# A hand-ordered passage from the O projection into the up projection of a float32 decoder layer

## The chip, the cores and the metric

One NeuronCore of one Trainium2 chip runs the program. The metric is the device time of one execution in microseconds (us); a time of a kernel is the median of its runs. Engines are named as the profile names them: PE (TensorE, matmuls), DVE (VectorE), ACT (ScalarE), POOL (GpSimd), SP (SyncE, which issues all DMAs here).

## What is computed

One layer of a decoder in float32, 1024 tokens by 1024 channels. Cut to what matters:

```python
def reference(x, ...):
    h = x
    u = rms_norm(h, attn_norm)
    h = h + swa_mixer(u, w_qkv, sinks, w_o)      # windowed attention; ends in "o @ w_o", the O projection
    u = rms_norm(h, mlp_norm)                    # statistics over the channels of each token
    a = jax.nn.relu(u @ w_up)                    # w_up 1024 x 4096, the up projection
    h = h + (a * a) @ w_down                     # the down projection
    return rms_norm(h, final_norm)
```

## The kernel before

Activations lie transposed: 8 tiles `h[m]` of 128 channels by 1024 tokens, and the tokens are taken in two halves of 512 columns. Every float32 matmul is made of three: an operand is split into a rounded part (`_h`, a copy on ACT) and a rest (`_l`, a subtraction on DVE), and `mm3b` multiplies high by high, high by low and low by high into one PSUM bank.

**The O projection's second part** runs 16 blocks (8 channel tiles by 2 halves) of 12 matmuls. After each block DVE adds it into `h[m]`, ACT squares the result, and POOL (tiles 1 to 4) or DVE (tile 5) adds up the squares. `stat_sum(hf)` sums them over channels with small matmuls (`n2s`) and makes the reciprocal root (`n_st`, ACT and DVE) and a diagonal tile `dg`; `stat_bcast(hf)` spreads it over the partitions with a matmul (`n2b`). Half 0 is normed while half 1 is still projected (`norm_first`, giving `x1_i` and its split `xb`).

**The up projection** uses a seven-product scheme (Winograd's form of Strassen's) on 2 by 2 blocks: the columns of `w_up` are taken as 16 pairs `p`, and for each the products 1 to 7 of weight terms and activation terms are formed (`TERM`). A product (n, p) is four channel groups i of three matmuls. Products 1 and 2 need only half 0 (`xb`). The others need the terms `t1` and `t2` (`ta`, split into `xt`), `t3` and `t4` (split into `xu`) and `b22` (split into `xc`), which mix both halves: per group i, `norm_second` norms the two tiles of half 1 into a new tile (two scalar_tensor_tensor), subtracts twice for `ta`, splits it, has POOL make the two differences for t3 and t4 in place of `x1_i`, and splits `xc`. Weight sums (`sa`, `sb`) come from POOL (`up_sums`), their splits `ws`, `wb`, `wt` from `up_splits`.

Results are taken out of PSUM after most products: (1,p) and (6,p) are copied by ACT, (2,p) is added by DVE into `oa` and squared-relu'd (`relu2`, one DVE instruction), and so on; each result is stored to DRAM (`hid`) by SP. PSUM has three banks X, two Y, one Z and two mm: (1), (6), (7), (4) of one p share a bank X, (5) and (3) a bank Y, (2) a bank Z.

**What sets the order.** The matmuls are always in program order (`pe.ordered`). DVE, ACT and POOL are ordered by hand only through the attention (`Ordered`); from there on the build's scheduler places their instructions, by program order as priority and by its own estimate of when each is ready. Each engine then runs its list strictly in turn. Tiles come from small pools (tags A 16 tiles, Q 8, O 6, W 6, K 4, R 3 for raw weights, t4 6 for temporaries, sq 4), and an instruction that needs a slot waits until its last reader is done. The products run as (1,0), (2,0), (1,1), (2,1), (1,2), (2,2), (1,3), (2,3), (6,0), (5,0), (6,1), (5,1), (7,0), (6,2), (4,0), (3,0), (7,1), (5,2), (6,3), (4,1), (3,1) and so on. Line 41, which nearly all rows carry, is the `Ordered` wrapper, so rows are told apart by their tiles.

Of the kernel before, what the change touches and what calls it, by code (L numbers as in the profile page):

```python
# [62 lines left out]
def trunk(tc, xT, gains, wqkv, wo, wup, wdn, bias_d, sinks_d, ident_d, mask_d, outT):  # L63
# [602 lines left out]
    def xalloc(dt, name):
        return xslots.pop(0)(dt, name)

    def norm_second(i, rb):
# [5 lines left out]
        for m in (2 * i, 2 * i + 1):
            d = nc.sync.dma_start(hd[m], h[m])
            tc.add_manual_dep(d.ins, stt.ins.name, mybir.DependencyInfo(
                mybir.DependencyClass.Sync, mybir.DependencyReason.DATA), reason="order")
# [6 lines left out]
        XP["b22", i] = split1(xt[:, 1], xalloc, f"xc{i}")  # L685

    def norm_third(i):
        XP["t3", i], XP["t4", i] = split2(x1[i], xalloc, f"xu{i}")

    def ring():  # L690
        tags, n = [wtile] * 6 + [otile] * 6, [0]
# [36 lines left out]

    PS, OUT = {}, {}
# [6 lines left out]
    def up_product(n, p):  # L736
# [21 lines left out]
        if n == 1:
            s.copy(c11, ps)
        elif n == 2:  # L760
            v.tensor_tensor(c11, ps, c11, op=ALU.add)
            relu2(c11, c11)
            store(2, c11)
        elif n == 6:
            s.copy(OUT["b", p][:, 0], ps)
# [40 lines left out]
    for hf in range(2):
        for m in range(KT):
            ps = bank(obanks[(hf * KT + m) % 5], f"o1_{m}_{hf}")
            for kk in range(4):
                mm3(ps, wsl(ws[m // 2], (m % 2) * 4 + kk), o_t[4 + kk], HALVES[hf], kk == 0, kk == 3)  # L810
            v.tensor_tensor(h[m][:, HALVES[hf]], ps, h[m][:, HALVES[hf]], op=ALU.add)
            square(m, hf)
            if hf == 1 and m == 1:
                stat_sum(0)
            if hf == 1 and m == 3:
                rb = stat_bcast(0)
            if hf == 1 and m > 3:
                norm_first(m - 4, rb)
# [220 lines left out]
```

## Time and profile before

| | |
|---|---|
| median of 3 runs | 956.98 us (955.43 to 957.41) |
| the profiled execution's own time | 957.42 us, its span 955.7 us |
| PE busy | 920.7 us of the span (96%) |
| DVE, ACT, POOL busy | 689.4, 441.3, 313.1 us |

The profile has one page (busy times, the span in 40 slices of 23.9 us, the costliest groups) and views asked of the trace: a timeline of one engine (start, duration, what was done, and in brackets how long the engine sat idle before and who released it), groups of instructions, and busy times of chosen stretches. The attention ends near 249 us, the O projection's second part at 296 us, the up projection near 633 us, and the down projection follows. A matmul's duration overlaps the next one's, so its price is the distance from start to start.

### The profile page before, as it was taken

The page shows a single profiled execution, that of the slowest core. Times are in us where ns is not written, and L with a number is a line of the kernel's source. Part 1 is how long each engine was busy: PE and PEld are TensorE (multiplying, and loading weights), DVE is VectorE, ACT ScalarE, POOL GpSimd, SP SyncE. Part 2 cuts the span into 40 slices and gives each one's busy share as a digit, 9 for nine tenths or more (in the row PEclk, how much of TensorE's full clock was granted, in tenths as well). Part 3 has the DMA queues.
Part 4 walks back from the last instruction along what each step waited for, and adds up shares of the span by engine and source line. Part 5 has one row for each costly group of instructions (what it writes and reads, how often), then busy time and mean ns, then how long its engine had stood idle before and what let it go on. Part 6 is the DMA issues. An engine that isn't in the chain of part 4 may idle for free.

```text
span 955.7 us, 12587 instructions
## 1 busy us (share of the span) xinstructions
PE 920.7 (96%) x4500; PEld 772.5 (81%) x4500; DVE 689.4 (72%) x947; ACT 441.3 (46%) x837; POOL 313.1 (33%) x266
## 2 busy tenths in 40 slices
PE   7999999999999859999999999999999999999996
PEld 5778888888887647888888888878888888888995
DVE  6779988989746886776657665555868697467963
ACT  8478878777533343433333333333343333455510
POOL 4116656566361265544544454110000000030100
PEclk9999999999998969999999999999999999999998
DMA  8200100510410424555345533799898989447722
GB/s 301 69 23 28 56 27 8 204 45 25 153 45 23 167 100 174 176 168 170 126 144 169 173 127 140 260 311 390 292 328 312 341 327 342 131 132 246 282 89 88
DMA packets 56174, 160.36 MB, mean 168 GB/s; under 512 B 6320, under 2 KB 10160, under 8 KB 56112
## 3 DMA queue, kind: packets, MB, share of 16 engines
q1 hardware_dynamic: 56112, 159.57, 47.4%
q8 instruction: 35, 0.57, 0.2%
q14 instruction: 27, 0.22, 0.1%
HBM read 121.79 MB, written 37.75 MB: 167 GB/s over the span
## 4 chain that ended last, share of the span: by engine, by line
PE 60%; DVE 1%; POOL 1%; issue 0%; ACT 0%; DVEq 0%; ACTq 0%; POOLq 0%
PE d L41 32%; PE uX L41 15%; PE uY L41 8%; PE uZ L41 3%; POOL sa L41 0%; POOL sb L41 0%; DVE out L41 0%; PE n L41 0%; PE n3b L41 0%; DVE wb L41 0%; DVE hr L41 0%; DVE ws_l L41 0%; ACT oc L41 0%; ACT ws_h L41 0%; ACT wt_h L41 0%
## 5 line engine op out<-in xcount | busy, mean ns | idle before, releaser
L41 PE MATMUL d<-dx_h,dw_h 128*128 128x512 f32 (+1 forms) x512 | 186.8, 365 | 1.0 <-DVE hr L41 1.0
L41 PE MATMUL d<-dx_l,dw_h 128*128 128x512 f32 (+1 forms) x512 | 185.9, 363 | 0.0
L41 PE MATMUL d<-dx_h,dw_l 128*128 128x512 f32 (+1 forms) x512 | 185.9, 363 | 0.0
L41 PEld LDWEIGHTS d<-dx_h,dw_h 128*128 128x128 f32 x512 | 96.7, 189 | 16.6 <-DVE hr L41 1.4
L41 PEld LDWEIGHTS d<-dx_l,dw_h 128*128 128x128 f32 x512 | 96.7, 189 | 15.2 <-issue 0.2
L41 PEld LDWEIGHTS d<-dx_h,dw_l 128*128 128x128 f32 x512 | 96.7, 189 | 15.0
L41 ACT CAST dw_h<-wf 128x1024 fp32r<-128x1024 f32 x40 | 42.1, 1053 | 112.4 <-PE d L41 64.9
L41 POOL TENSOR_TENSOR ssq3a<-ssq3a,sq_a 128x512 f32<-128x512 f32 x7 | 10.8, 1544 | 212.9 <-ACT sq_a L41 212.5
L41 DVE TENSOR_TENSOR dx_l<-hr,dx_h 128x1024 fp32r<-128x1024 f32 x56 | 70.3, 1256 | 6.1 <-ACT dx_h L41 6.1
L41 DVE TENSOR_TENSOR dw_l<-wf,dw_h 128x1024 fp32r<-128x1024 f32 x40 | 49.2, 1231 | 27.3 <-ACT dw_h L41 27.3
L41 POOL TENSOR_TENSOR t<-t,sm 128x512 f32<-128x512 f32 x32 | 33.3, 1041 | 102.9 <-DVE sm L41 102.9
L41 DVE TENSOR_TENSOR wf<-wd,we 128x1024 f32<-128x1024 f32 x40 | 48.3, 1221 | 25.0 <-DMA we<-wdn 17.5
L41 ACT CAST dx_h<-hr 128x1024 fp32r<-128x1024 f32 x56 | 58.6, 1047 | 10.9 <-DMA hr<-hid 6.3
L41 ACT ACTIVATE t<-t,sm 128x129 f32<-128x129 f32 x128 | 50.5, 397 | 11.0 <-DVE sm L41 10.5
L41 PE MATMUL f<-xh,w_h 128*128 128x512 f32 x128 | 53.7, 420 | 0.0
L41 PE MATMUL f<-xl,w_h 128*128 128x512 f32 x128 | 50.9, 397 | 0.0
L41 PE MATMUL f<-xh,w_l 128*128 128x512 f32 x128 | 50.5, 395 | 0.0
L41 ACT COPY oa<-uX 128x512 f32<-128x512 f32 x32 | 18.8, 587 | 61.1 <-PE uX L41 61.1
L41 POOL TENSOR_TENSOR ob<-ob,oa 128x512 f32<-128x512 f32 x16 | 20.6, 1289 | 80.4 <-DVE ob L41 80.4
L41 POOL TENSOR_TENSOR oc<-oc,oa 128x512 f32<-128x512 f32 x16 | 22.6, 1411 | 69.4 <-DVE oc L41 69.4
L41 PE MATMUL uX<-xu_h,wb 128*128 128x512 f32 x128 | 42.2, 391 | 0.7 <-ACT oa L41 0.7
L41 DVE TENSOR_TENSOR oc<-oc,oa 128x512 f32<-128x512 f32 x16 | 13.0, 813 | 38.1 <-ACT oc L41 38.0
(341 smaller groups left out, 2454.5 us busy)
## 6 DMA issues: line engine op xcount, KB each, us to landing
wd<-wdn SPq DMA_DIRECT2D x56, 512.0 KB, 6.0
hr<-hid SPq DMA_DIRECT2D x56, 512.0 KB, 4.9
we<-wdn SPq DMA_DIRECT2D x40, 512.0 KB, 6.8
hid<-oa SPq DMA_DIRECT2D x32, 256.0 KB, 3.0
hid<-oc SPq DMA_DIRECT2D x32, 256.0 KB, 2.3
hid<-ob SPq DMA_DIRECT2D x32, 256.0 KB, 2.3
w_r<-wqkv SPq DMA_DIRECT2D x8, 512.0 KB, 3.9
h<-xT SPq DMA_DIRECT2D x8, 512.0 KB, 6.4
```

Of the source, the lines that this page charges most:

```text
L41: ins = method(*args, **kw)
```

## The change

- From the second half of the O projection's blocks to the product (6,2), DVE, ACT and POOL run in program order; the program order there is rewritten line by line, with the split of a tile into its `_h` copy and its `_l` subtraction placed apart.
- `stat_sum(0)` comes one block after the first half's last (it was two), `stat_bcast(0)` one block later (it was three), and the four `norm_first` steps two or more blocks before the end. `stat_sum(1)` is put inside product (1,0), after its third group, and `stat_bcast(1)` inside (2,0), after its third.
- `second_half` norms half 1 in place of `h`, so `h` is stored to `hd` before, in 16 stores of half a tile rather than 8.
- The differences for t3 and t4 go from POOL to DVE and come after all `ta`. The relu and square of (2,0) to (2,3) go from one DVE instruction to two on ACT, after product (5,1). The `xc` splits come after the ordered part.
- `wb` of p 0 and 1 is split ahead of the O projection; the weight sums of p 2 are made in place of the raw weights and one `sq` tile, ahead of the products; those of p 3 come with (7,1). Tags of some tiles change.
- The products' order from (6,2) on is (6,2), (7,0), (7,1), (4,0), (3,0), (5,2), (4,1), (6,3), (3,1), (7,2), (5,3), (4,2), (3,2), (7,3), (1,4), (4,3), (2,4), (3,3); from p 4 on it is unchanged.

No matmul is added or taken away. The core of the diff is below. In it `his` makes the `_h` copy on ACT and returns the function that makes the `_l` subtraction on DVE; `t34(i)` and `t34_lo(i)` do the same for `xu` of group i; `c11_add` is DVE's addition of (2,p) into `oa`; `snapshot` is ACT's copy of (1,p) or (6,p); `up_mms` is a product's matmuls alone, with functions called after given groups.

```diff
+    def second_half(i, rb):
+        for m in (2 * i, 2 * i + 1):
+            hm = h[m][:, HALVES[1]]
+            v.scalar_tensor_tensor(hm, hm, gn[:, 1, m:m + 1], rb, op0=ALU.mult, op1=ALU.mult)
+    def t_sums(i):
+        ta = (temp if i < 2 else lambda n: two(atile(F32, n)))(f"ta{i}")
+        v.tensor_tensor(ta[:, 1], h[2 * i][:, HALVES[1]], x1[i][:, 0], op=ALU.subtract)
+        v.tensor_tensor(ta[:, 0], h[2 * i + 1][:, HALVES[1]], ta[:, 1], op=ALU.subtract)
+        return ta
-        g.tensor_tensor(x1[i][:, 0], ta[:, 0], x1[i][:, 0], op=ALU.subtract)
-        g.tensor_tensor(x1[i][:, 1], x1[i][:, 1], ta[:, 0], op=ALU.subtract)
+    def t3_sum(i):
+        v.tensor_tensor(x1[i][:, 0], TA[i][:, 0], x1[i][:, 0], op=ALU.subtract)
+    def t4_sum(i):
+        v.tensor_tensor(x1[i][:, 1], x1[i][:, 1], TA[i][:, 0], op=ALU.subtract)
+    def c11_relu(p):
+        c11 = OUT["a", p][:, 0]
+        s.activation(c11, c11, AF.Relu)
+        s.activation(c11, c11, AF.Square)
+        store(2, p, c11)
...
+    for e in (v, s, g):
+        e.ordered = True
+    for m in range(KT):
+        ps = oblock(m, 1)
+        if m == 1:
+            rb = stat_bcast(0)
+        if 2 <= m < 5:
+            LO[m - 1] = first_half(m - 1, rb)
+        if 2 <= m < 6:
+            XP["b11", m - 2], XP["b21", m - 2] = LO[m - 2]()
+        if m == 6:
+            WU["s2", 0], WU["s1", 0] = LO["ws0"]()
+        oadd(m, 1, ps)
+        if m == 0:
+            stat_sum(0)
...
+        if m == 1:
+            LO[0] = first_half(0, rb)
+        if m == 5:
+            LO["ws0"] = his(SUM[0][1], wtile, "ws0")
+        if m == 6:
+            LO["wt0"] = his(SUM[0][2], wtile, "wt0")
...
+    s2_2 = up_sums_inplace(2, *u2)
+    WU["s3", 0], WU["s4", 0] = LO["wt0"]()
+    up_mms(1, 0, {2: lambda: stat_sum(1)})
+    LO["wa3"] = his(wu3, ktile, "wa3")
+    snapshot(1, 0)
+    WU["a11", 3], WU["a12", 3] = LO["wa3"]()
+    bc = []
+    up_mms(2, 0, {2: lambda: bc.append(stat_bcast(1))})
+    rb = bc[0]
+    second_half(0, rb)
+    LO["ws1"] = None
+    for p in range(4):
+
+        if p < 3:
+            c11_add(p)
+        TA[p] = t_sums(p)
+        LO[p] = his(TA[p], atile, f"xt{p}")
+        if p == 3:
+            t3_sum(0)
+            XP["t2", p], XP["t1", p] = LO[p]()
+            t4_sum(0)
+            break
+        up_mms(1, p + 1)
+        snapshot(1, p + 1)
+        if p == 1:
+            LO["ws1"] = his(SUM[1][1], otile, "ws1")
+        second_half(p + 1, rb)
+        XP["t2", p], XP["t1", p] = LO[p]()
+        up_mms(2, p + 1)
...
+    t34(0, atile)
+    up_mms(6, 0)
+    WU["s2", 1], WU["s1", 1] = LO["ws1"]()
+    t3_sum(1)
+    t4_sum(1)
+    snapshot(6, 0)
+    t34(1, ktile)
+    t34_lo(0)
+    up_mms(5, 0)
...
+    up_mms(6, 1)
+    snapshot(6, 1)
+    t3_sum(3)
+    t4_sum(3)
+    t34(2, atile)
+    t34(3, otile)
...
+    up_mms(5, 1)
+    t34_lo(3)
+    c11_relu(0)
+    up_product(6, 2)
+    LO["wt1"] = his(SUM[1][2], otile, "wt1")
+    WU["s3", 1], WU["s4", 1] = LO["wt1"]()
+    c11_relu(1)
+    c11_add(3)
+    for e in (v, s, g):
+        e.ordered = False
+    for i in range(4):
+        b22_split(i)
```

## Rows read from the trace of the kernel before

**Rows 1.** The page: busy time of each engine with its share of the span and count, and two lines of the 40 slices (tenths; PEclk is the granted clock of TensorE, in tenths of full speed).

```profile
PE 920.7 (96%) x4500; PEld 772.5 (81%) x4500; DVE 689.4 (72%) x947; ACT 441.3 (46%) x837; POOL 313.1 (33%) x266
...
PE   7999999999999859999999999999999999999996
...
PEclk9999999999998969999999999999999999999998
```

**Rows 2.** Stretches from the first product (1,0) on: bounds, length, busy time of each engine (with counts), granted clock of TensorE, share of DMA, GB/s.

```profile
298.28:301.68 3.40, 1.29 (x5) 0.68 (x5) 1.86 (x2) 1.46 (x2) 0.00 (x0) 0.98 0.00 0
301.68:306.65 4.97, 4.97 (x25) 4.97 (x24) 0.00 (x0) 0.58 (x1) 0.00 (x0) 0.50 0.01 3
306.65:311.85 5.20, 5.20 (x13) 4.11 (x14) 1.43 (x6) 0.38 (x2) 0.00 (x0) 0.51 0.00 0
...
326.37:331.74 5.37, 4.42 (x19) 3.30 (x18) 5.37 (x6) 2.05 (x3) 2.99 (x2) 1.00 0.85 302
331.74:352.81 21.07, 8.62 (x19) 5.54 (x19) 18.28 (x19) 7.59 (x9) 11.13 (x7) 0.59 0.32 125
...
372.10:374.04 1.94, 0.50 (x3) 0.30 (x3) 1.91 (x3) 0.58 (x1) 0.40 (x1) 1.00 0.34 131
374.04:640.00 265.96, 265.29 (x1170) 219.48 (x1169) 170.92 (x187) 92.80 (x125) 117.48 (x79) 1.00 0.52 176
```

**Rows 3.** PE's timeline: the column sums of half 0 and the matmul behind them; the first matmul of (2,2) and the first of (1,3), twelve matmuls later.

```profile
276.30 2.73 PE L41 MATMUL n2s<-ones,sq 128*128 128x1 f32 x24
278.90 0.49 PE L41 MATMUL o<-oh,wo_h 128*128 128x512 f32 x1
...
320.93 0.39 PE L41 MATMUL uZ<-xb_h,wa_h 128*128 128x512 f32 x1
...
323.65 0.39 PE L41 MATMUL uX<-xb_h,wa_h 128*128 128x512 f32 x1
```

**Rows 4.** PE's timeline: five matmuls that waited.

```profile
299.79 0.50 PE L41 MATMUL uX<-xb_h,wa_h 128*128 128x512 f32 x1 [1.35 <-ACT xb_h L41]
...
327.49 0.51 PE L41 MATMUL uZ<-xb_h,wa_h 128*128 128x512 f32 x1 [0.95 <-DVE oa L41]
...
335.84 0.79 PE L41 MATMUL uX<-xt_h,ws_h 128*128 128x512 f32 x1 [3.93 <-ACT xt_h L41]
339.45 0.79 PE L41 MATMUL uX<-xt_l,ws_h 128*128 128x512 f32 x1 [2.83 <-DVE xt_l L41]
...
373.70 0.50 PE L41 MATMUL uY<-xt_h,ws_h 128*128 128x512 f32 x1 [1.44 <-DVE ob L41]
```

**Rows 5.** DVE's timeline from one group's `xt_l` to the next one's.

```profile
328.67 2.31 DVE L41 TENSOR_TENSOR xt_l<-ta,xt_h 128x1024 fp32r<-128x1024 f32 x1
...
332.83 0.68 DVE L41 TENSOR_TENSOR ta<-x,x 128x512 f32<-128x512 f32 x1
333.43 0.68 DVE L41 SCALAR_TENSOR_TENSOR oa<-oa 128x512 f32<-128x512 f32 x1
334.03 0.68 DVE L41 TENSOR_TENSOR ta<-x,ta 128x512 f32<-128x512 f32 x1
...
335.23 1.97 DVE L41 TENSOR_TENSOR wt_l<-sb,wt_h 128x1024 fp32r<-128x1024 f32 x1
337.12 2.28 DVE L41 TENSOR_TENSOR xt_l<-ta,xt_h 128x1024 fp32r<-128x1024 f32 x1
```

**Rows 6.** Groups of DVE's instructions from 300 to 345 us: busy time, mean ns of one, idle time before them.

```profile
L41 DVE TENSOR_TENSOR xt_l<-ta,xt_h 128x1024 fp32r<-128x1024 f32 x4 | 9.1, 2284 | 0.0
L41 DVE SCALAR_TENSOR_TENSOR x<-h,gn,n2b 128x512 f32<-128x512 f32 x8 | 5.6, 739 | 1.1 <-PE n2b L41 1.1
L41 DVE TENSOR_TENSOR oa<-uZ,oa 128x512 f32<-128x512 f32 x4 | 2.7, 684 | 3.4 <-PE uZ L41 3.4
...
L41 DVE TENSOR_TENSOR xb_l<-x,xb_h 128x1024 fp32r<-128x1024 f32 x1 | 1.2, 1226 | 0.8 <-ACT xb_h L41 0.8
```

**Rows 7.** Groups of POOL from 300 to 372 us (the differences for t3 and t4), then of ACT from 300 to 600 us (a copy out of PSUM, the square of `oc`, a high part).

```profile
L41 POOL TENSOR_TENSOR x<-x,ta 128x512 f32<-128x512 f32 x4 | 8.5, 2126 | 0.0
L41 POOL TENSOR_TENSOR x<-ta,x 128x512 f32<-128x512 f32 x4 | 6.0, 1491 | 41.3 <-DVE ta L41 41.3
...
L41 ACT COPY oa<-uX 128x512 f32<-128x512 f32 x29 | 17.0, 587 | 56.0 <-PE uX L41 56.0
L41 ACT ACTIVATE oc<-oc 128x512 f32<-128x512 f32 x14 | 8.8, 632 | 0.4
L41 ACT CAST xt_h<-ta 128x1024 fp32r<-128x1024 f32 x4 | 4.2, 1048 | 14.9 <-DVE ta L41 14.9
```

**Rows 8.** The statistics of half 1 behind the column sums that ended at 306.65 us: ACT's root, and DVE's diagonal.

```profile
306.83 0.26 ACT L41 ACTIVATE n_st<-n2s,eps 128x4 f32<-128x4 f32 x1 [4.33 <-PE n2s L41]
...
308.00 0.69 DVE L41 TENSOR_TENSOR dg<-ident,n_st 128x512 f32<-128x512 f32 x1
```

**Rows 9.** The weights of p 3: SP's issue of the second raw half, POOL's first sum, DVE's rest of `ws`; and DVE's add of (3,0), behind which the bank Y of (5,2) came free.

```profile
356.93 0.33 SPq L715 DMA_DIRECT2D wu3b<-wup  x1
...
360.29 1.29 POOL L41 TENSOR_TENSOR sb<-wu3c,wu3b 128x512 f32<-128x512 f32 x1 [3.39 <-DVE wt_l L41]
...
370.13 1.22 DVE L41 TENSOR_TENSOR ws_l<-sa,ws_h 128x1024 fp32r<-128x1024 f32 x1
...
372.97 0.68 DVE L41 TENSOR_TENSOR ob<-uY,ob 128x512 f32<-128x512 f32 x1
```

More of the change, by code (lines that the diff above doesn't have):

```diff
@@ L687, in norm_third, with his, los @@
[L687 to L691, printed above, removed]
+            ins = v.scalar_tensor_tensor(out[:, e], h[m][:, HALVES[hf]], gn[:, 1, m:m + 1], rb,
+                                         op0=ALU.mult, op1=ALU.mult)
+        return ins
+    def his(src, alloc, name):
+        hi, lo = two(alloc(F32R, f"{name}_h")), two(alloc(F32R, f"{name}_l"))
+        s.copy(hi, src)
+        def los():
+            v.tensor_tensor(lo, src, hi.bitcast(F32), op=ALU.subtract)
+            return [(hi[:, i], lo[:, i]) for i in range(2)]
+        return los
@@ L803, in trunk @@
         up_sums(p, None, lambda name: two(ktile(F32, name)))
+    for p in range(2):
+        WU["a22", p] = split1(SUM[p][0][:, 1], wtile, f"wb{p}")
     obanks = ["mm", "X", "mm", "X", "X"]
-    rb = None
[L806 to L818, printed above, removed]
@@ L839, in trunk, with oblock @@
-    for p in range(1, EARLY):
-        order += [(7, p)] + ([(5, p + 1)] if p + 1 < EARLY else [(1, EARLY)]) + [(4, p)]
-        order += [(3, p)] if p + 1 < EARLY else [(2, EARLY), (3, p)]
-        if p + 2 < EARLY:
-            order.insert(len(order) - 2, (6, p + 2))
+    TA, LO = {}, {}
+    def oblock(m, hf):
+        ps = bank(obanks[(hf * KT + m) % 5], f"o1_{m}_{hf}")
+        for kk in range(4):
+            mm3(ps, wsl(ws[m // 2], (m % 2) * 4 + kk), o_t[4 + kk], HALVES[hf], kk == 0, kk == 3)
+        return ps
@@ new lines, in oadd @@
+    def oadd(m, hf, ps):
+        v.tensor_tensor(h[m][:, HALVES[hf]], ps, h[m][:, HALVES[hf]], op=ALU.add)
+        square(m, hf)
+    for m in range(KT):
+        oadd(m, 0, oblock(m, 0))
+    for e in (v, s, g):
+        e.ordered = True
+    rb = None
+    for m in range(KT):
+        ps = oblock(m, 1)
[11 more added lines that the diff above has]
+            for i in range(4):
+                stored(i, 0)
+            wu3 = two(rtile("wu3a"))
+            nc.sync.dma_start(wu3, wup[3, 0])
+            u2 = up_load(2)
+        if m == 1:
[4 more added lines that the diff above has]
+            LO["wt0"] = his(SUM[0][2], wtile, "wt0")
+        if m % 2 == 1:
+            stored(m // 2, 1)
@@ new lines, in t34, with t34_lo @@
+    def t34(i, alloc):
+        LO["xu", i] = his(x1[i], alloc, f"xu{i}")
+    def t34_lo(i):
+        XP["t3", i], XP["t4", i] = LO["xu", i]()
+    t34(0, atile)
[7 more added lines that the diff above has]
+    up_mms(5, 0)
+    t3_sum(2)
+    t4_sum(2)
+    walloc = ring_up()
+    s2h, s1h = walloc(F32R, "ws2_h"), walloc(F32R, "ws2_l")
+    s2h, s1h = two(s2h), two(s1h)
+    s.copy(s2h[:, 0], s2_2)
```

140 lines of the change are left out of this document (75 added, 65 removed).

## The prediction

> **What bounds the kernel now.** I read the page first, for the engine that fills the span and for the slices in which it doesn't. PE is busy 96% of it, and the 40 slices show one hole away from the ends: two slices near 310 to 360 us, where the granted clock dips too [rows 1]. So PE sets the end, and a change is worth what it takes out of that hole. Next I cut the hole into stretches at the matmuls that waited [rows 2, 4] and asked what PE had to do in each. Twelve matmuls of a product take 2.72 us from start to start where nothing holds them, 0.227 each, and the column sums take 2.60 at the full clock [rows 3]. Over and above that the stretches lost:
>
> - 298.28 to 301.68, three matmuls (0.68): 2.72 lost, waiting for `xb` of group 3.
> - 301.68 to 306.65, the column sums: 4.97 - 2.60 = 2.37 lost. The granted clock is 0.50, that is 1.2 GHz; the waits just before let it fall.
> - 306.65 to 311.85, product (2,0), still at 0.51: 5.20 - 2.72 = 2.48 lost.
> - 326.37 to 331.74, eighteen matmuls (4.08): 1.29 lost, bank Z waiting for DVE's add [rows 4].
> - 331.74 to 352.81, seventeen matmuls (3.86): 17.21 lost, on `xt_h` and `xt_l` of groups 2 and 3, the tail of it at half clock.
> - 372.10 to 374.04, one matmul: 1.71 lost, bank Y waiting for DVE.
>
> The sum is 27.8 us. After 374 us PE is busy 265.29 of 265.96 us [rows 2], so what is saved before moves the end, and nothing behind gives anything back. That is the ceiling.
>
> The cause of the largest term stands in DVE's queue: from one group's `xt_l` to the next group's are 337.12 - 328.67 = 8.45 us [rows 5]. In them lie a relu, a weight split and others that nothing on PE is waiting for, beside the two `ta`. And `xt_l` takes 2.28 us, where the same shape takes 1.23 as `xb_l` [rows 6]; the former run while POOL makes the t3 and t4 differences, which themselves spread from 1.5 to 2.1 us [rows 7].
>
> **The change, part by part.** All prices of DVE are places in its queue: a 512-wide instruction 0.60 (starts at 332.83, 333.43, 334.03 [rows 5]; durations overlap by 0.08), one with the gain and the broadcast 0.739 - 0.08 = 0.66, a 1024-wide rest 1.23 - 0.08 = 1.15 [rows 6].
>
> *Half 0 earlier.* Its `xb` steps are placed two or more blocks ahead of the end, so the 2.72 goes. DVE then has to do in the six last blocks (6 x 2.72 = 16.3 us) four pairs of norms (5.3), four `xb_l` (4.6), six adds and a square sum (4.2), one or two weight rests (1.2 to 2.4): 15.3 to 16.5. It just fits, and is the tight spot: ACT's last square, behind the `wt0` copy that waits for a W tile, may come late for the column sums.
>
> *Statistics inside the products.* From the end of the column sums to the end of `dg` are 308.69 - 306.65 = 2.04 us [rows 8]. Behind the sums PE has the last group of (1,0) and three of (2,0), twelve matmuls, 2.72. So chain and broadcast are hidden with 0.7 to spare, and without a wait ahead of the sums the clock should stay up, as in the sums of half 0 (2.60 [rows 3]). So 2.37 and 2.48 go. I leave 0.5 for a late square (bounds 0 and 1.5, plus 4.85 if the clock falls all the same).
>
> *The loop over p.* Per round DVE has c11_add 0.60, two `ta` 1.20, two norms 1.32, one `xt_l` 1.15: 4.27, against two products on PE, 5.44. The bank Z is added first in its round, one product before it is needed, so the 1.29 goes. In-place norms wait for the stores of `h`; those are issued block by block, and the last have more than two products' time, so I cost them at nothing. An issue holds SP for 0.33 [rows 9], so the 16 are 5.3 us of a queue that in the O projection has three loads besides.
>
> *The end of the chain.* From the end of (2,2): 0.2 to DVE (PE's end to ACT's root is 0.18 [rows 8]), then 0.60 + 1.20 + 1.32 + 1.15 + 1.20 = 5.47 to the last `ta`, ACT's copy 1.05 [rows 7], the rest 1.23 and 0.2 for two handovers: 8.15. PE reaches the use of that rest after two products, nine matmuls and one: 5.44 + 2.04 + 0.23 = 7.71. A wait of 0.45 is left of 17.21; I take 0.5, with bounds 0 and 2.5 (two splits that the scheduler slips in ahead).
>
> *Differences on DVE.* Eight on DVE cost 8 x 0.60 = 4.8. POOL loses 14.5 [rows 7], and the four `xt_l` lose 4 x 1.05. From the last `ta` to the rest of `xu` of group 3 DVE has ten 512-wide (6.0) and six 1024-wide (6.9): 12.9, which ends 5.67 + 12.9 + 0.4 = 19.0 us after (2,2). PE wants it in (7,0) after seven products and nine matmuls, 21.1. Spare 2.1, unless POOL's sums for p 3 run beside it and take 1.05 from each of four rests; I take 0.5, bounds 0 and 4.
>
> *Relus on ACT.* Four go from 0.60 on DVE to two of about 0.63 on ACT [rows 7], an engine with 46% of the span. They stand ahead of one PSUM copy, in time that ACT has free: nothing. The Trainium skill, page "ScalarE: Activation LUTs", section "Rules for kernel authors", advises VectorE for relu, as the faster; here the trace agrees on the price of one, but DVE is the queue that others wait for. By the rule the four would stay on DVE, 2.4 us against the 2.1 that it has to spare above, and the sum would be 0.3 more.
>
> *`wt1` for (7,1).* ACT copies (6,2) first (0.59), then `wt1_h` 1.05, then DVE 1.23, with handovers 3.1 us after (6,2); (7,1) wants the rest 2.72 + 0.45 = 3.17 after it. I take 0.5, bounds 0 and 1.1 (a rest of 2.28).
>
> *(5,2) behind (3,0).* It needs the bank Y of (3,0), and now no product stands between: at least 0.2 + 0.68 + 0.1 = 1.0. Before, the add came 1.71 + 2.72 = 4.4 us behind [rows 2, 9], being queued. Four `xc` rests and two evacuations are in DVE's queue at that time, so between 1.0 and 4.4 I take 2.0. This term is new in size: it was 1.71.
>
> *(6,3) and the weights of p 3.* From SP's load to the rest of `ws` were 371.35 - 356.93 = 14.4 us [rows 9]. The slot for the load comes free at the earliest with the rest of p 2's s1, 16.3 us after (2,2) by the queue above; (6,3) comes thirteen products after (2,2), 35.4 plus some 3 of waits. Spare: 7.7, less what the split of `wb` of p 2 waits in the unordered part behind `xc` splits and relus. I take 1.0, bounds 0 and 8.
>
> *POOL's in-place sums of p 2* run before the products with nothing behind them; they may stretch two DVE rests by 1.05 each, inside the 0.5 of the statistics.
>
> Sum of waits left: 0.5 + 0.5 + 0.5 + 0.5 + 2.0 + 1.0 = 5.0. Gain 27.8 - 5.0 = 22.8. The profiled execution took 957.42, 0.44 over the median of 956.98, so 934.6 on its own scale and **934.2 us** for the median.
>
> **The rivals.** *Weights of p 3 late (943.7).* The chain of 14.4 us starts only when DVE has worked off the unordered splits, (6,3) waits the 8, and the next product runs at half clock (2.48): 934.2 + 7.0 + 2.5. For it: three raw slots, and six temporaries that results, sums and differences share. Against: PE has thirteen products in hand.
>
> *The clock falls at the column sums (939.1).* 4.85 come back. For it: that is what the rows show for half 1; against: those for half 0, with dense matmuls ahead, kept it.
>
> *Slower than before (964).* The fixed order makes every round a little too long, each product of the twelve from (2,0) to (6,2) waits, and PE never gets its clock back: 12 x 2.48 = 29.8 on top of 934.2. It decides from the point where DVE's round exceeds PE's 5.44, that is, if two rests take 2.28 and a split slips in (4.27 + 1.05 + 1.15 = 6.5). For it: in 331.74 to 352.81 waits of 2.8 to 3.9 us between few matmuls held the mean clock at 0.59 [rows 2, 4]. Against: POOL is idle in those rounds, and single waits of 0.95 and 1.44 left the clock of their stretches at 1.00. [...]
>
> *No change (957).* If the hole were not the queue but the latency of `ta`, copy and rest, order would not help. But that latency is 1.2 + 1.05 + 1.23, a third of the 8.45.
>
> **How the numbers follow.** Forecast 0.71, weights of p 3 late 0.12, clock at the sums 0.08, slower 0.05, no change 0.04. The range: at the low end only the 1.0 of (5,2) is left, 957.0 - 26.8 = 930.2; at the high end late weights and (5,2) at near its bound, 945. It leaves out the last two, and a little at the edges. Faster by over 0.2% (about what a measurement of this kernel tells from no change) 0.91, within 0.04, slower 0.05.
>
> **What would show it.** Right: PE without a wait over 1 us from 296 to 335 us and PEclk at full; column sums of half 1 at 2.6 us; `xt_l` near 1.23; a wait on DVE's `ob` ahead of (5,2); up projection's end near 610 us. Wrong, step by step: a wait in the sums (squares late), on `xt_l` in (6,0) over 2.5 us, on `xu_l` in (7,0), on `ws` in (6,3), or DVE idle behind an instruction that waits for a slot. The forecast as a whole fails if the clock drops and the products' spacing shows 5.20 / 12 = 0.43 for 0.227.

## The result and the profile after

The changed kernel takes **945.22 us** (median of 4 runs, 944.47 to 946.90) against 956.99 beside it (955.43 to 957.41): ratio 0.9882, interval 0.9865 to 0.9900. It is faster, by 11.8 us where 22.8 were forecast, and 945.2 lies just above the range's end of 945. The profiled execution took 945.41 us, its span 943.7. The page:

```profile
PE 917.3 (97%) x4500; PEld 769.9 (82%) x4500; DVE 689.2 (73%) x952; ACT 445.7 (47%) x846; POOL 297.2 (31%) x258
...
PE   7999999999989998999999999999999999999996
...
PEclk9999999999999999999999999999999999999998
```

Against [rows 1] the slice at 5 tenths, whose clock was at 6, is filled, and two single 8s are left away from the ends. Stretches, cut at the matmuls that waited (columns as in [rows 2]):

```profile
279.05:284.35 5.30, 2.69 (x6) 1.18 (x5) 2.85 (x6) 1.77 (x3) 0.96 (x1) 0.74 0.94 252
284.35:302.81 18.46, 18.46 (x82) 15.28 (x81) 17.50 (x20) 8.32 (x11) 7.87 (x7) 0.98 0.33 128
302.81:309.81 7.00, 7.00 (x37) 6.10 (x36) 3.79 (x8) 3.25 (x5) 3.32 (x2) 0.76 0.23 82
309.81:329.72 19.91, 19.91 (x87) 16.14 (x86) 16.80 (x24) 7.87 (x10) 0.00 (x0) 1.00 0.10 37
...
373.63:384.00 10.37, 10.37 (x39) 8.37 (x40) 7.82 (x10) 3.30 (x6) 1.62 (x2) 0.84 0.48 168
384.00:640.00 256.00, 255.32 (x1127) 211.10 (x1126) 162.98 (x176) 91.80 (x121) 106.19 (x72) 1.00 0.53 184
```

PE's timeline, the column sums of half 1 and the matmuls that still waited:

```profile
282.05 1.22 PE L41 MATMUL n2b<-dg,ones 128*128 128x512 f32 x1 [2.61 <-DVE dg L41]
...
302.81 2.73 PE L41 MATMUL n2s<-ones,sq 128*128 128x1 f32 x24
...
330.70 0.50 PE L41 MATMUL uX<-xt_l,ws_h 128*128 128x512 f32 x1 [0.59 <-DVE xt_l L41]
...
349.55 0.50 PE L41 MATMUL uX<-xu_h,wb 128*128 128x512 f32 x1 [1.77 <-ACT oa L41]
...
356.86 0.50 PE L41 MATMUL uY<-xt_h,ws_l 128*128 128x512 f32 x1 [1.58 <-DVE ob L41]
...
373.63 0.69 PE L41 MATMUL uY<-xt_h,ws_h 128*128 128x512 f32 x1 [2.85 <-DVE ob L41]
```

What a stretch loses is its length less 0.227 us for each matmul due in it (and 2.60 for the sums): 4.4 us from 279.05 to 284.35 (the broadcast of half 0, four matmuls), 1.7 from 302.81 to 309.81 (no wait, but the clock near 1.2 GHz behind the sums), 0.8 at (6,0), 1.9 at (4,0), 1.7 at (5,2), and 3.0 + 1.7 at (5,3) and in the half clock behind it: 15.2 us. The forecast had left 5.0.

What was forecast for the rounds happened. DVE's groups from 309 to 345 us:

```profile
L41 DVE SCALAR_TENSOR_TENSOR h<-h,gn,n2b 128x512 f32<-128x512 f32 x8 | 5.6, 742 | 2.3 <-PE n2b L41 2.3
L41 DVE TENSOR_TENSOR xt_l<-ta,xt_h 128x1024 fp32r<-128x1024 f32 x4 | 4.9, 1220 | 0.5 <-ACT xt_h L41 0.5
```

`xt_l` takes 1.22 us where it took 2.28 [rows 6], and from 309.81 to 329.72 PE is busy all the time.

The two largest losses were not forecast at all, and each is a queue in which something stands ahead that PE doesn't need yet. First, DVE's queue ahead of `dg` of half 0, then ACT's and POOL's in the same time:

```profile
277.12 0.17 DVE L41 RECIPROCAL n_st<-n_st 128x4 f32<-128x4 f32 x1
277.32 1.04 DVE L41 TENSOR_TENSOR n_st<-n_st 128x4 f32<-128x4 f32 x1
278.39 0.16 DVE L41 SCALAR_TENSOR_TENSOR n_st<-n_st 128x4 f32<-128x4 f32 x1
279.90 0.69 DVE L41 TENSOR_TENSOR wb<-wu0b,wb 128x512 fp32r<-128x512 f32 x1 [1.34 <-ACT wb L41]
280.51 0.69 DVE L41 TENSOR_TENSOR wb<-wu1b,wb 128x512 fp32r<-128x512 f32 x1
281.11 0.16 DVE L41 SCALAR_TENSOR_TENSOR n_st<-n_st 128x4 f32<-128x4 f32 x1
281.30 0.69 DVE L41 TENSOR_TENSOR dg<-ident,n_st 128x512 f32<-128x512 f32 x1
...
279.25 0.62 ACT L41 CAST wb<-wu0b 128x512 fp32r<-128x512 f32 x1 [2.24 <-PE o L41]
...
277.05 1.29 POOL L41 TENSOR_TENSOR sb<-wu1c,sa 128x512 f32<-128x512 f32 x1
```

ACT's `wb` waits 2.24 us for a matmul of the O projection, whose weights hold the W tile, DVE's two rests wait for ACT, and the last step of the root and `dg` stand behind them. Second, ahead of (5,3), DVE, ACT and POOL:

```profile
371.75 1.23 DVE L41 TENSOR_TENSOR ws_l<-sa,ws_h 128x1024 fp32r<-128x1024 f32 x1 [6.23 <-ACT ws_h L41]
372.89 0.68 DVE L41 TENSOR_TENSOR ob<-uY,ob 128x512 f32<-128x512 f32 x1
...
370.67 1.05 ACT L41 CAST ws_h<-sa 128x1024 fp32r<-128x1024 f32 x1 [6.75 <-POOL sa L41]
...
362.12 1.61 POOL L41 TENSOR_TENSOR oc<-oc,oa 128x512 f32<-128x512 f32 x1 [4.77 <-DVE oc L41]
...
365.62 1.29 POOL L41 TENSOR_TENSOR sb<-wu4a,wu4b 128x512 f32<-128x512 f32 x1 [0.65 <-DMA hid<-od]
...
369.35 1.29 POOL L41 TENSOR_TENSOR sa<-wu4b 128x512 f32<-128x512 f32 x1
```

DVE sits idle for 6.23 us at the weights of p 4, while the add of (3,1) behind them is all that (5,3) needs. In the kernel before, the scheduler had that add ahead of the same rest, and (5,3) didn't wait:

```profile
385.09 0.68 DVE L41 TENSOR_TENSOR ob<-uY,ob 128x512 f32<-128x512 f32 x1
...
387.01 1.21 DVE L41 TENSOR_TENSOR ws_l<-sa,ws_h 128x1024 fp32r<-128x1024 f32 x1
```

### The profile page after: what moved, and what is told of

It is laid out like the page before. It is cut to its first block, busy times and chain, and to the rows that moved or that the text cites. A ratio compares the mean times of both kernels' runs of the same rounds, so it can differ in the third digit from the quotient of the medians.

```text
span 943.7 us, 12589 instructions
## 1 busy us (share of the span) xinstructions
PE 917.3 (97%) x4500; PEld 769.9 (82%) x4500; DVE 689.2 (73%) x952; ACT 445.7 (47%) x846; POOL 297.2 (31%) x258
## 4 chain that ended last, share of the span: by engine, by line
PE 88%; DVE 6%; ACT 2%; issue 2%; DMA 1%; POOL 1%; SPq 0%; DVEq 0%; ACTq 0%
PE d L41 33%; PE uX L41 16%; PE f L41 12%; PE uY L41 9%; PE o L41 5%; PE uZ L41 4%; PE pv L41 3%; PE S L41 3%; PE pt L41 1%; DVE xl L41 1%; DMA xr<-xT 1%; PE n2s L41 1%; DVE oa L41 1%; DMA hid<-od 1%; DVE t L41 1%
## 5 line engine op out<-in xcount | busy, mean ns | idle before, releaser
L41 PEld LDWEIGHTS d<-dx_h,dw_h 128*128 128x128 f32 x512 | 96.6, 189 | 16.5 <-DVE hr L41 1.4
L41 POOL TENSOR_SCALAR_AFFINE_SELECT cur<-hl 128x1024 fp32r<-128x1024 f32 x32 | 39.5, 1235 | 2.0 <-DVE hl L41 2.0
```

The lines of the kernel that those rows point to most:

```text
L41: ins = method(*args, **kw)
```

## The experiments

Each kernel ran beside runs of the kernel before, so they are compared by their ratios to it; the changed kernel's is 0.9882, and a thousandth is 0.96 us. Executions differ by 2 us already ahead of the passage (the sums of half 0 begin at 273.82 us here, at 271.47 in e1's), so what a place loses is read within one trace.

**Moving one wait each.** e1_wb_later moves the two splits off the queue ahead of `dg`:

```diff
-    for p in range(2):
-        WU["a22", p] = split1(SUM[p][0][:, 1], wtile, f"wb{p}")
...
+        if m == 2:
+            for p in range(2):
+                WU["a22", p] = split1(SUM[p][0][:, 1], wtile, f"wb{p}")
         if m == 5:
```

> One edit to the changed kernel: the two splits of wb (p 0 and 1) go from ahead of the O projection to behind the third block of half 1, inside the ordered part. Theory: in the changed kernel PE waits 2.6 us for dg of half 0 and then runs at half clock for some matmuls, 6.4 us in all, because DVE's queue has the two wb rests between the root and dg, and these wait for a W tile that comes free only when the block has ended in front of which dg is wanted. Moved away, dg is ready about when PE wants it: the wait shrinks below 1 us, up to 6 us come back, and the 1.2 us of the two rests now stand in the way of the last squares, so 939.5 to 941.5. Rival: the wait is the root's own latency (table load, POOL beside it) and the splits only fill idle time: 944 to 945.5.

944.02 us, 0.9869 (0.9855 to 0.9882): 1.2 us, within the intervals. The broadcast of half 0 no longer waits, but the sums of half 1 do, and then run near 1.2 GHz (granted clock 0.57 from 299.2 to 302.6 us). PE's timeline, and DVE's at the first rest of `wb`:

```profile
296.83 1.02 PE L41 MATMUL n2s<-ones,sq 128*128 128x1 f32 x8 [0.52 <-DVE sq L41]
299.20 3.33 PE L41 MATMUL n2s<-ones,sq 128*128 128x1 f32 x16 [1.34 <-ACT sq L41]
...
283.71 1.44 DVE L41 TENSOR_TENSOR wb<-wu0b,wb 128x512 fp32r<-128x512 f32 x1 [1.27 <-ACT wb L41]
```

DVE's queue in half 1 had no room for them, as the prediction's 15.3 to 16.5 us of work for 16.3 lets expect: with an idle 1.27 us for ACT's copy the two rests took some 3 us there, the last two adds began 20.8 us behind the broadcast for 19.4, and most of the gain was given back.

e2_p4_later puts the weights of p 4 ahead of (7,2), not (6,3):

```diff
-        if (n, p) == (7, 1) or (n == 6 and p >= EARLY - 1):
+        if (n, p) in ((7, 1), (7, 2)) or (n == 6 and p >= EARLY):
...
-            while ready <= min(max(p + 1, 3), NG - 1):
+            while ready <= min(3 if n == 7 and p == 1 else max(p + 1, 4), NG - 1):
```

> One edit to the changed kernel: the weights of p 4 come into the program ahead of (7,2) rather than of (6,3). That takes DVE's rest of ws of p 4 from ahead of the add of (3,1) to behind it. Theory: (5,3) waits 2.85 us for bank Y since that add stands in DVE's queue behind a rest whose operand is not there, and the clock then falls for about 2 us more: both go, 940 to 941.5. Rival: bank Y is late since DVE has too much to do there: the wait stays or moves to a neighbour, 944 to 946.

940.76 us, 0.9835 (0.9815 to 0.9855): 4.5 us. No wait of (5,3) on `ob` is left, so the cause of that wait is shown. The size is less certain: in e2's profiled execution the clock also stayed up behind the sums of half 1, which has nothing to do with the edit and was 1.7 us in the changed kernel's.

e3_relu_later moves the relus of p 2 and 3 on ACT behind (3,0):

```diff
-    for p in (2, 3):
-        c11_relu(p)
...
+        if (n, p) == (3, 0):
+            for q in (2, 3):
+                c11_relu(q)
```

> One edit to the changed kernel: the relus on ACT of p 2 and 3 come behind product (3,0) in the program; in ACT's queue those of p 3 then stand behind the PSUM copies of (7,0) and (7,1). Theory: (4,0) waits 1.8 us (2.3 with the matmuls after it) because ACT's copy of (7,0) stands behind relus and splits; with two relus and a split of xc out of the way 1.6 us come back, 943.6. Rival: DVE is the next in line there, and the wait turns up at (5,2) or (3,0): 945.

943.68 us, 0.9866 (0.9851 to 0.9881): 1.5 us, within the intervals. The wait at (4,0) falls from 1.77 to 0.21, that at (5,2) grows from 1.58 to 2.59, as the rival said, and that at (5,3) falls from 2.85 to 1.25; the number is the theory's.

e4_swap takes (4,1) ahead of (5,2):

```diff
-    order = [(7, 0), (7, 1), (4, 0), (3, 0), (5, 2), (4, 1), (6, 3), ...
+    order = [(7, 0), (7, 1), (4, 0), (3, 0), (4, 1), (5, 2), (6, 3), ...
```

> One edit to the changed kernel: (4,1) and (5,2) change places, so that a product stands between (3,0) and (5,2). Theory: (5,2) waits 1.9 us for bank Y only because (3,0) is right in front of it: 943.3. Rival: DVE's add of (3,0) is late by its queue, or the next bank Y is then late (one product fewer between (3,1) and (5,3) is not the case, but the queue is the same): 945.

940.29 us, 0.9832 (0.9819 to 0.9845): 4.8 us, more than the wait that it was meant for. (5,2) and (5,3) no longer wait, and (4,2) loses 1.3 us.

e5_all makes all four edits.

> The four edits together: the wb splits behind block 3 of half 1, the weights of p 4 ahead of (7,2), the relus of p 2 and 3 behind (3,0), and (4,1) ahead of (5,2). If their gains were independent: 945.2 - 1.2 - 4.5 - 1.5 - 4.9 = 933. Theory: the second and the fourth both remove the wait of 3 us plus half clock at (5,3), which counts once, and the third's gain went to (5,2): 937 to 939 us. Rival (what is postponed all falls together behind (3,0) and makes a new wait on wt or ws there): 941 or more.

942.78 us, 0.9861 (0.9845 to 0.9876): the rival. Four gains that came to 12 us one by one are 2 together. The sums of half 1 wait as in e1, and there is a wait at (4,2) that is much smaller in e2 (0.34 us) and e4 (1.13). PE's and ACT's timeline:

```profile
373.15 0.50 PE L41 MATMUL uX<-xu_h,wb 128*128 128x512 f32 x1 [3.41 <-ACT oa L41]
...
371.57 1.04 ACT L41 CAST ws_h<-sa 128x1024 fp32r<-128x1024 f32 x1 [6.40 <-POOL sa L41]
372.52 0.58 ACT L41 COPY oa<-uX 128x512 f32<-128x512 f32 x1
```

The copy of (7,2) stands behind the `ws_h` of p 4 on ACT, which waits for POOL. So the wait moved from DVE's queue to ACT's; the order is the same in e2 and e4, where POOL's sum came sooner for PE.

**Undoing one part each.** u0_unordered leaves out the hand order itself:

```diff
-    for e in (v, s, g):
-        e.ordered = True
     rb = None
     for m in range(KT):
```

> DVE, ACT and POOL are no longer held to program order from the second half of the O projection on; the rewritten program order, the new tiles and all else stay. Theory (the gain over the kernel before is carried by the hand order): the scheduler slips splits and relus between the steps of norm, ta and xt_l again, a round on DVE passes PE's 5.44 us, and waits on xt_l come back: 950 to 957 us. Rival (the new program order as priority is enough, and the two wb rests now fall behind dg by themselves): 939 to 944 us, the wait of 2.77 us ahead of the broadcast of half 0 gone.

939.39 us, 0.9825 (0.9810 to 0.9841): the theory fell. 16.6 us are gained without the fixed order, 5.5 more than with it by the ratios. The `wb` rests now stand behind `dg`, (4,0) and (5,3) don't wait, (6,0) waits 0.82 us for 0.59, the sums of half 1 now 0.92, and (5,2) more:

```profile
355.01 0.50 PE L41 MATMUL uY<-xt_h,ws_l 128*128 128x512 f32 x1 [3.43 <-DVE ob L41]
```

u1_pool gives the differences back to POOL:

```diff
-        v.tensor_tensor(x1[i][:, 0], TA[i][:, 0], x1[i][:, 0], op=ALU.subtract)
+        g.tensor_tensor(x1[i][:, 0], TA[i][:, 0], x1[i][:, 0], op=ALU.subtract)
...
-        v.tensor_tensor(x1[i][:, 1], x1[i][:, 1], TA[i][:, 0], op=ALU.subtract)
+        g.tensor_tensor(x1[i][:, 1], x1[i][:, 1], TA[i][:, 0], op=ALU.subtract)
```

> The eight differences for t3 and t4 go back from DVE to POOL, at the places they have in program order. Theory of the prediction: POOL needs 14.5 us for them behind the last ta, the rests of xt and xu that run beside them take up to 2.28 us where they took 1.22, and the rest of xu of group 3 comes 1.5 to 3 us later than (7,0) wants it: 947 to 949 us, with a wait on xu in (7,0). Rival (DVE is relieved of 4.8 us and what is queued behind it, among it the adds that (4,0), (5,2) and (5,3) wait for, comes earlier): 941 to 944 us. If both cancel: 945.

948.63 us, 0.9922 (0.9909 to 0.9935): the theory's number, but not its way. POOL starts each pair as soon as its `ta` is there, in the rounds, and (7,0) doesn't wait for `xu`. Nor did the rests of the chain slow down as priced: `xt_l` takes 1.25 us in the mean with POOL's differences beside it, and it is POOL's instruction, begun just behind, that gets longer. The loss is at (5,2). DVE and POOL in the first round, then PE and DVE at (5,2):

```profile
313.00 1.23 DVE L41 TENSOR_TENSOR xt_l<-ta,xt_h 128x1024 fp32r<-128x1024 f32 x1
...
313.10 2.28 POOL L41 TENSOR_TENSOR x<-x,ta 128x512 f32<-128x512 f32 x1
...
360.97 0.79 PE L41 MATMUL uY<-xt_h,ws_l 128*128 128x512 f32 x1 [6.37 <-DVE ob L41]
...
356.66 1.31 DVE L41 TENSOR_TENSOR ws_l<-sa,ws_h 128x1024 fp32r<-128x1024 f32 x1 [3.48 <-ACT ws_h L41]
...
360.24 0.68 DVE L41 TENSOR_TENSOR ob<-uY,ob 128x512 f32<-128x512 f32 x1
```

The scheduler, free again by then, now put p 3's weights ahead of the add of (3,0), which in the changed kernel began first (356.13 us for `ws_l`'s 356.77): the same head of queue that p 4's weights are for (5,3).

u3_stats_back puts the sums of half 1 behind (1,0) and the broadcast behind (1,1):

```diff
-    up_mms(1, 0, {2: lambda: stat_sum(1)})
+    up_mms(1, 0, {3: lambda: stat_sum(1)})
...
-    up_mms(2, 0, {2: lambda: bc.append(stat_bcast(1))})
-    rb = bc[0]
+    up_mms(2, 0)
+    c11_add(0)
+    up_mms(1, 1)
+    snapshot(1, 1)
+    rb = stat_bcast(1)
...
```

> The column sums of half 1 stand behind the whole of (1,0), and the broadcast behind (1,1), so 3.4 us later in PE's order than in the changed kernel; nothing else moves but c11_add(0), which comes ahead of the norms. Theory (the chain behind the broadcast bounds PE at (6,0), where the wait is 0.75 us): the wait at (6,0) grows to 2.5 to 4 us and the clock falls behind it: 947 to 950 us. Rival (the rounds have 5.44 against 4.27 us and catch up, or the squares, no longer hurried, keep the clock up at the sums): 943 to 945.5 us.

946.51 us, 0.9897 (0.9881 to 0.9913): 1.4 us slower, between the two expectations, and the intervals overlap. The wait on `xt_l` at (6,0) is 0.76 us for 0.59; putting the statistics inside the products rather than one product later is worth little.

x3_relu_dve gives all four relus back to DVE, right behind the adds:

```diff
             c11_add(p)
+            relu2(OUT["a", p][:, 0], OUT["a", p][:, 0])
...
-    c11_relu(0)
+    store(2, 0, OUT["a", 0][:, 0])
...
```

> The relu and square of (2,0) to (2,3) go back from two ACT instructions to one on DVE, each right behind the add of its bank Z, the first three inside the rounds; the stores stay. Theory (DVE's queue is what others wait for, and its rounds were emptied for that): 0.66 us more at the end of the chain, so the wait at (6,0) goes from 0.75 to about 1.4 us, and xu_l for (7,0) comes 2.6 us later, at its bound: 946 to 948 us. Rival (a round has 5.44 us and holds 4.27, so 0.66 fits, and ACT, relieved of eight instructions, makes the copies for (4,0) without a wait): 942 to 944 us.

943.72 us, 0.9860 (0.9844 to 0.9875): 2.1 us less. Each was half right: (6,0) waits 1.0 us in two pieces for 0.59, as the theory said, and (4,0) no longer waits; (5,3) doesn't either, but (4,2) now waits 2.40 us for ACT's copy. The Trainium skill, page "ScalarE: Activation LUTs", section "Rules for kernel authors", would leave relu on VectorE; the trace agrees here by the median, though the intervals overlap.

**Two edits together.** f1_swap_unordered is u0_unordered with e4_swap's order.

> Two edits that each gained alone: the engines left unordered from the second half of the O projection on (939.4 alone) and (4,1) ahead of (5,2) (940.3 alone). Theory: the unordered kernel's largest loss in the passage is 3.6 us ahead of (5,2), and the product (4,1) of 2.7 us put in front covers most of it, with the half clock behind: 934.5 to 936.5 us. Rival (the add that (5,2) waits for, or an ACT copy for (4,1), is late whatever stands in front, as with the four edits together): 938 to 940 us.

938.89 us, 0.9818 (0.9805 to 0.9831), the rival's 938 to 940: (5,2) loses 1.1 us for 3.6, and (5,3) now 2.3.

f2_stats_swap keeps the hand order, has e4_swap's order, and spreads the work of DVE in half 1:

```diff
...
         if m == 1:
+            for p in range(2):
+                WU["a22", p] = split1(SUM[p][0][:, 1], wtile, f"wb{p}")
             LO[0] = first_half(0, rb)
...
-    WU["s3", 0], WU["s4", 0] = LO["wt0"]()
+    WU["s2", 0], WU["s1", 0] = LO["ws0"]()
     up_mms(1, 0, {2: lambda: stat_sum(1)})
-    LO["wa3"] = his(wu3, ktile, "wa3")
+    LO["wt0"] = his(SUM[0][2], wtile, "wt0")
     snapshot(1, 0)
-    WU["a11", 3], WU["a12", 3] = LO["wa3"]()
+    WU["s3", 0], WU["s4", 0] = LO["wt0"]()
...
+        if p == 0:
+            LO["wa3"] = his(wu3, ktile, "wa3")
+            WU["a11", 3], WU["a12", 3] = LO["wa3"]()
...
```

> The hand order is kept. The wb splits come behind block 1 of half 1 (DVE is idle there, waiting for the broadcast), and so that DVE has no more to do before the column sums of half 1 than in the changed kernel, the rest ws_l of p 0 comes behind the last add, the wt split of p 0 behind the first root, and the split of p 3's first weights into the first round; (4,1) stands ahead of (5,2). Theory (the wait for dg and the late squares of the first experiment are one surplus of DVE work in half 1, and it can be moved to where DVE idles): no wait at the broadcast of half 0, none or under 0.5 us at the column sums of half 1: 945.2 - 4.8 - 4.9 = 935.5 us, 934 to 937. Rival (the rounds are too full with the split of 1.2 us, or the sums wait all the same): 938 to 941 us. If the clock falls behind the column sums of half 1 with no wait ahead of them, as in the changed kernel, the sums themselves let it fall.

939.14 us, 0.9824 (0.9808 to 0.9839): the rival. `dg` is in time, but the sums still lose 1.1 us, and the split in the first round makes bank Z wait 1.4.

f3_stats_swap_relu adds e3_relu_later's edit.

> As f2_stats_swap, and the relus of p 2 and 3 behind (3,0). Theory: the wait of 1.9 us at (4,0) goes, and with (4,1) ahead of (5,2) it has no second place to come back: 1.5 us less than f2_stats_swap, about 934. Rival (the ACT copies or DVE adds behind (3,0) are late in its place, as when the relus alone were moved): the same as f2_stats_swap within 0.8 us, or worse.

940.42 us, 0.9836 (0.9820 to 0.9852), no better: the rival. (4,0) waits 0.21 us for 1.77, and (4,2) loses 2.1 us for 1.1.

**The clock behind the column sums.** s1_spread cuts each half's 24 sums into three pieces:

```diff
...
-        for i, sq in enumerate(parts):
-            colsum(ps, sq, 4, i == 0, i == len(parts) - 1)
...
+    def stat_part(hf, i):
+        if i == 0:
+            stat["ps", hf] = bank("Y", f"n2s{hf}")
+        colsum(stat["ps", hf], stat["sq", hf][i], 4, i == 0, i == 2)
...
+            if part and kk > 0:
+                stat_part(0, kk - 1)
...
-    up_mms(1, 0, {2: lambda: stat_sum(1)})
+    up_mms(1, 0, {0: lambda: stat_part(1, 0), 1: lambda: stat_part(1, 1),
+                  2: lambda: (stat_part(1, 2), stat_sum(1))})
```

> The changed kernel with the 24 column sums of each half no longer in one piece: eight stand behind each of three stretches of three to six matmuls (half 0 inside the first block of half 1, half 1 behind the first three groups of (1,0)). Theory (2.7 us of 128x1 matmuls in one piece let the clock fall for some 4 us behind them, in some executions and not in others): granted clock 1.00 behind both sums, and the median of the runs 1 to 2 us lower: 943 to 944.5. Rival (the fall comes from something else, such as what was queued before): the clock falls behind half 1 as in the changed kernel, 945.

s2_double makes each sum of half 1 twice:

```diff
-            colsum(ps, sq, 4, i == 0, i == len(parts) - 1)
+            if hf:
+                colsum(ps, sq, 4, i == 0, False)
+            colsum(ps, sq, 4, i == 0 and not hf, i == len(parts) - 1)
```

> The changed kernel with every column sum of half 1 made twice into the same bank (48 instead of 24 in one piece), so the statistics of half 1 are doubled. Theory (the piece of 128x1 matmuls itself lets the clock fall): it falls to 1.2 GHz within the second half of the piece, in every execution; 2.6 us for the sums, some more for their own half clock and 2 us behind: 949 to 952 us. Rival (the sums do not matter for the clock): 945.2 + 2.6 = 947.8.

s1_spread took 941.79 us, 0.9843 (0.9829 to 0.9857), 3.7 us less than the changed kernel, twice what was expected; s2_double 950.91, 0.9943 (0.9929 to 0.9957), 5.8 more. Stretches (the clock is the third figure from the end) of e3_relu_later (half 0: one piece and behind it), s1_spread (half 1: sums and behind them), s2_double (half 1: first half, second half, behind):

```profile
273.20:275.80 2.60, 2.60 (x26) 2.60 (x24) 0.69 (x1) 1.60 (x2) 2.60 (x3) 1.00 0.03 10
275.80:279.40 3.60, 3.60 (x12) 2.85 (x12) 1.57 (x4) 0.58 (x2) 1.98 (x2) 0.58 0.18 19
```

```profile
297.94:302.30 4.36, 4.27 (x32) 3.64 (x30) 2.90 (x4) 2.10 (x3) 4.36 (x3) 1.00 0.33 124
302.30:306.30 4.00, 4.00 (x18) 2.96 (x18) 2.65 (x8) 1.69 (x3) 0.76 (x1) 1.00 0.00 0
```

```profile
304.14:306.74 2.60, 2.60 (x26) 2.60 (x24) 1.22 (x1) 1.10 (x2) 2.60 (x2) 1.00 0.43 168
306.74:311.46 4.72, 4.72 (x27) 4.72 (x26) 0.00 (x0) 0.00 (x0) 0.35 (x1) 0.55 0.00 0
311.46:316.00 4.54, 4.54 (x12) 3.57 (x13) 2.56 (x7) 1.78 (x3) 0.00 (x0) 0.50 0.10 20
```

Behind one piece of 2.6 us, with dense matmuls and no wait ahead, the clock fell in some profiled executions and not in others (behind half 1 in the changed kernel's, behind half 0 in e3's and e4's, behind neither in e2's); doubled, it fell within the piece; in three pieces it stayed at 2.4 GHz. The theory holds. But not all of the 3.7 us is this clock: in s1's trace the waits at (5,2) and (5,3) are 0.78 and 2.14 us for 1.58 and 2.85, and as s2 has the same two with one doubled piece, they don't come from the spreading.

s3_swap_unord_spread and s4_stats_swap_spread are f1 and f2 with the sums in three pieces, those of half 1 one group later; s4 also takes p 3's split out of the first round:

```diff
+    LO["wa3"] = his(wu3, ktile, "wa3")
+    WU["a11", 3], WU["a12", 3] = LO["wa3"]()
     bc = []
```

> As f1_swap_unordered (938.9), with the column sums in three pieces; those of half 1 behind the second, third and fourth group of (1,0), so that the last square, 0.9 us late there, has one group more. Theory: the wait of 1.09 us and the fall of the clock behind the sums both go: 936 to 937.5. Rival (the chain behind the broadcast, now 0.7 us later, gives it back at (6,0)): 938 to 939.

> As f2_stats_swap (939.1), the column sums in three pieces as in s3_swap_unord_spread, and the split of p 3's first weights not in the first round but ahead of the norms, while DVE waits for the broadcast. Theory: the waits of f2_stats_swap at the column sums (1.1 us) and at bank Z (1.6 us) go, and the clock stays: 935.5 to 937. Rival (each saved wait comes back at the next place where DVE or ACT is late, (4,0) to (5,3)): 938.5 or more.

937.36 us (934.72 to 940.84), 0.9801 (0.9782 to 0.9821), and 936.94 (936.37 to 940.97), 0.9805 (0.9787 to 0.9824): over 7 us under the changed kernel, and the lowest medians of the study. Their intervals still overlap with those of f1 and f2, but single executions go to 934.7 where f1's fastest took 938.7. An execution's time goes with its mean granted clock: in s3 934.7 us at 0.997 and 940.8 at 0.990, in s4 936.4 at 0.996 and 941.0 at 0.988. s4's profiled execution still loses 1.9 us ahead of the broadcast of half 0, 1.3 at the sums of half 1, 0.8 at (6,0), 1.9 at (4,0) and 1.2 at (4,2). s5_root_first and s6_root_relu_dve go for the first and the fourth; ACT's queue in s4 shows why `dg` is late with no split ahead:

```profile
274.98 0.64 ACT L41 ACTIVATE sq<-h 128x512 f32<-128x512 f32 x1 [3.92 <-DVE h L41]
275.63 1.28 ACT L41 ACT_TABLE_LOAD   x1
276.93 0.26 ACT L41 ACTIVATE n_st<-n2s,eps 128x4 f32<-128x4 f32 x1
```

```diff
-        oadd(m, 1, ps)
         if m == 0:
             stat_sum(0)
+        oadd(m, 1, ps)
```

> As s4_stats_swap_spread, with the root of half 0 ahead of the add and the square of block 0 of half 1. In s4_stats_swap_spread the order is add, square (ACT 274.98), table load (275.63, 1.28 us), root (276.93), while the sums ended at 274.95, and the broadcast loses 1.9 us. Theory (the square, and the table load that it holds back, are the head of queue): the table load falls under the sums, the root follows at once, dg is 2 us earlier and the wait goes: 935 to 936 us. Rival (the add and square, now 2 us later, come back as late squares at the sums of half 1): 936.5 to 938.

> As s5_root_first, with all four relus on DVE as in x3_relu_dve. Theory (ACT's copies for (4,0) stand behind relus, worth 1.9 us there against 0.7 more at (6,0)): 1 to 1.5 us less than s5_root_first, near 934.5. Rival (as with x3_relu_dve, where (4,2) lost 2.6 us for 1.2): the same as s5_root_first within 0.8 us.

942.18 us, 0.9846 (0.9832 to 0.9860), and 944.71, 0.9875 (0.9859 to 0.9891): worse than both rivals. In s5 the table load runs under the sums and the broadcast doesn't wait, so the cause was right. But the adds and squares of half 1 did not come earlier by as much: the sums wait 1.76 us for 1.18 in s4, and behind this wait the clock falls even with the sums in three pieces, as it did not in s4 (1.00 from 299.53 to 305.70 us). s5, PE's timeline and the stretches from 302 us:

```profile
299.71 1.06 PE L41 MATMUL n2s<-ones,sq 128*128 128x1 f32 x8 [1.76 <-DVE sq L41]
```

```profile
302.00:306.00 4.00, 4.00 (x18) 3.65 (x16) 0.10 (x1) 0.00 (x0) 2.45 (x2) 0.50 0.11 43
306.00:312.00 6.00, 6.00 (x17) 4.59 (x18) 4.02 (x9) 2.63 (x4) 0.00 (x0) 0.60 0.00 0
```

In s6, (4,0) is free, and (4,2) loses 4.5 us at ACT's copy.

## Why the prediction was wrong by half

**Right in its largest terms.** The 17.21 of `xt_h` and `xt_l` became 0.8 at (6,0) (0.5 forecast); the waits for `xb` and bank Z are gone, and so is the half clock in the sums themselves (2.59 us); (5,2) loses 1.7 (2.0); (6,3) and (7,1) don't wait, `xt_l` is back at 1.22. In all, the terms that were charged with 5.0 came to 2.5.

**Wrong in the sum of waits left:** the step that failed is that only six waits were charged, 5.0 us in all, and four places outside of them lost 12.7 us. Less the 2.5 charged too much that is 10.2, against the 11.0 by which the gain fell short (the rest lies outside of the stretches). That 945.2 comes near the rival "weights of p 3 late" (943.7) is chance, since (6,3) doesn't wait.

- The `wb` splits ahead of the O projection were told as part of the change, and no price was set on them: 4.4 us at the broadcast of half 0. "*Half 0 earlier*" asked only whether `xb` came in time, not `dg`. Moving them alone brought 1.2 us (e1), and starting the root earlier cost 4 against s4 (s5): what leaves the broadcast comes back at the sums of half 1. This tight spot was named rightly; the 0.5 charged for it was not lost in the changed kernel itself, where the sums don't wait.
- "After 374 us ... what is saved before moves the end, and nothing behind gives anything back" failed: the weights of p 4 came 15 us earlier than before (`ws_l` at 371.75 for 387.01), but the scheduler, free again there, now put DVE's add for (5,3) behind them: 4.7 us (neither e2 nor e4 has this wait).
- Relus on ACT, "nothing": 1.9 us at (4,0), since ACT's PSUM copies stood behind relus, splits and high parts (e3, x3).
- The clock at the sums, bounded at "4.85 if the clock falls all the same", was not in the sum, and 1.7 were lost in the profiled execution, for a reason other than the prediction's: there was no wait ahead, it was the sums themselves (s1, s2).

**Right for a wrong reason: the hand order.** The prediction let the fixed order carry the gain; without it, the new program order gave 16.6 us in place of 11.8 (u0). A fixed order costs where a late instruction holds up those behind it; the scheduler put `dg` ahead of the `wb` rests by itself. With the work of half 1 placed anew the fixed order does as well (s4, 936.9 us, against 937.4 for s3 without it). And differences on DVE, priced at 2.1 us to spare for (7,0), decided nothing there, nor do they explain `xt_l`'s 1.22 us, since it takes 1.25 with them on POOL; what they changed was the order behind (u1).

Open: why the clock falls behind one piece of sums in one execution and not in the next; and which of the other edits (norms in place, tiles, loads, the products' order) carry how much of the gain, since none of them was undone alone.

## What to carry to other kernels

When an order is fixed by hand, list for each wait of the bounding engine everything that stands ahead of its producer in that queue, and for each of these what it waits for itself; a weight split that waits for a tile or a sum is such a head of queue. A removed wait pays only up to the next instruction that is late: four edits that gained 1.2 to 4.8 us alone gained 2 together. Narrow matmuls in one long piece are worth cutting up between dense ones, and gains of single edits are to be read beside the spread of their runs, since the clock behind such a piece moves them by 2 us.

## What was not expected of the hardware

- Column sums, 24 matmuls of 128x1 in 2.6 us, can be followed by some 4 us at a mean granted clock of 0.53 (the changed kernel, 305.40 to 309.00) to 0.58 (e3) with no wait ahead; eight at a time kept it at 1.00 where nothing waited ahead (s1) and behind a wait of 1.18 us (s4), and not behind a wait of 1.76 us (s5).
- A 4-column `tensor_tensor` on DVE took 1.04 us (277.32 to 278.36) where the same step of half 1 took 0.16 (at 306.15): it ended with POOL's sum (277.05 to 278.34), while the `reciprocal` just ahead, begun beside the same POOL instruction, took 0.17. The 1024-wide rests show it both ways in u1: `xt_l`, begun at 313.00 ahead of POOL's difference at 313.10, took 1.23 and POOL's 2.28; `ws_l`, begun at 329.34 behind POOL's of 328.29, took 2.30. The Trainium skill, page "SBUF — State Buffer", section "Terms", says that VectorE and GpSimd share a port pair that one of them holds for its whole instruction; the trace agrees for the instructions with two operands in SBUF.
